# A hybrid image transformer: products in plain float32 in place of three products of split float32r parts

## Chip, cores, metric

The kernel runs on one core of a Trainium2 chip. The metric is the device time of one execution in microseconds, the median of three runs. Before the change it is 1892.42 us (1891.81 to 1893.7).

## What is computed

Two layers act on 512 image tokens ("l") and 256 context tokens ("c") of width 1024, all in float32. Cut to what matters:

```python
for l in range(2):
    need_ctx = l < 1                                  # layer 1 leaves the context as it is
    mod = silu(c) @ w_mod[l] + b_mod[l]               # shifts, scales, gates; the same for ctx
    h_l, h_c = modulate(rms_norm(x)), modulate(rms_norm(ctx))
    # token mixer: 2816 columns of w_in, split in eleven parts
    conv  = gated_short_conv(cb, cc, cx)              # 256 columns
    ret   = retention both ways, 4 heads of 64        # rq, rk, rv, two gates
    attn  = 8 heads of 64 on 2 key/value heads: keys in a window of 3 blocks of 128,
            plus 256 context tokens, plus a sink      # aq, ak, av
    x = x + g1 * (concat(conv, ret, attn) @ w_out[l])
    # 16 experts, each takes its 64 best tokens (32 of the context)
    a, u = xs @ w_gate[l, e], xs @ w_up[l, e]
    x = x + g2 * scatter((silu(a) * u) @ w_down[l, e] * gate)
    if need_ctx: ctx gets the same two updates
return rms_norm(x, final_g)
```

## The kernel before

Each layer has two stages. The **mixer stage** norms the tokens, turns them (features on partitions, `make_h`), multiplies by `w_in` in eleven projections of 256 columns (`proj`, in the order `ORDER`), runs attention (`attn_all`) and retention (`ret_gen`), and ends with the output projection (`out_proj`), the second norm, the router and the choice of tokens. In layer 0 the products with `w_mod` of both layers (`mod_gen`) lie in it too. The **expert stage** (`experts`) works through eight pairs of experts; the weights come through a ring of tiles of 2 MB (`Ring`), each pair needs 12 of them. `gate`, `up` and `down` multiply in column tiles of 32 columns (layer 0) or 64 columns (layer 1) of the array, so that two or four products stand in it at once (`lat_mm`, line 1133; `cx_mm`, line 1140). In layer 1 the tokens of a pair are gathered by a product with a one-hot matrix (`gather_pe`, line 1123) and a pair's result is added with another one-hot product (`add`, lines 1359 and 1360, and `last_pair`, lines 1165 and 1166); layer 0 scatters by DMA except for its last pair.

**Split products.** A product of the mixers is made of three. `split` (lines 275 and 276) rounds a float32 tile to float32r on ScalarE, H = round(src), and takes the rest L = src - H on VectorE or, every second time, on GpSimd. `mm3` (lines 354 to 356) adds H*H, L*H and H*L of the two operands into one PSUM tile. Weights are split two chunks at a time after their load (`split_w`, two buffers each for wH and wL); the tokens once per layer (`make_h`, lines 343 and 344); the mixers' results before the output projection (`split_m`, into mH and mL). Attention scores put H and L of a query on the two halves of the partitions and multiply by H of the keys (twice) and by L of the keys (lines 666, 667, 670, 671), the window's mask is added by a product of bfloat16 with the identity (lines 673, 675). The one-hot products take the result's two parts yH and yL.

The other products (retention, P times V at line 711, `w_mod` at line 201, experts, gather) are plain float32 already.

**Order.** Every engine runs its instructions in program order. In the mixer stage the program order comes from `weave`, which mixes the projections' steps with steps of attention, of retention and of `mod_gen` at fixed ratios; functions put in `later` (turning Q, K) run between a projection's chunks. Within the experts TensorE's order is written by hand. Loads are issued by SyncE in one queue; a load waits there until its tile is free. The `w_in`, `w_mod` and `w_out` loads share four tiles (`wraw`, `NW`). The ring has N0 + 4 + N2 = 1 + 4 + 3 tiles in layer 1 and 3 + N1 = 6 in layer 0; the first 3 or 4 of them open in the place of the mixers' tiles, in layer 0 before the second half of the output projection, when `split_m` is through (`ra_open`).

Of the kernel before, what the change touches and what calls it, by code (L numbers as in the profile page):

```python
# [23 lines left out]
F32R = mybir.dt.float32r  # L24
# [14 lines left out]
S2L = (11, 12)  # L39
# [5 lines left out]
NS = 2  # L45
# [5 lines left out]
SUB = 2  # L51
# [12 lines left out]
N0, N1, N2 = 1, 3, 3  # L64


def f32(ap):
    return ap.bitcast(F32)
# [21 lines left out]
def kernel(ctx_stack: ExitStack, tc: tile.TileContext, x, c, ctx, c_ctx, w_mod, b_mod, norm1_g,  # L90
# [23 lines left out]
    identb = cst.tile([128, 128], BF, name="identb")  # L114
    DVE.tensor_scalar(identb, jp, 0.0, None, op0=OP.is_equal)
    mprev = cst.tile([128, 128], BF, name="mprev")
    DVE.tensor_scalar(mprev, jp, 0.0, NEG, op0=OP.is_lt, op1=OP.mult)
    mnext = cst.tile([128, 128], BF, name="mnext")
# [67 lines left out]
    def mod_gen(l, wp, pp, groups):  # L186

        for b in groups:
# [4 lines left out]
            for k in range(KC):  # L193
                w = []
                for h in range(2):
                    w.append(wp.tile([128, 2, 512], F32, name="wm", tag="wraw", bufs=NW))
                    SP.dma_start(w[h], w_mod[l, 128 * k:128 * k + 128, 2048 * b + 1024 * h:2048 * b + 1024 * h + 1024]
                                 .rearrange("p (q n) -> p q n", q=2))
# [12 lines left out]
    def mod_half(wp, pp, hf):  # L211
# [5 lines left out]
        for k in range(0, KC, 2):  # L217
            ps = pp.tile([128, 512], F32, name="ps_mod", tag="t", bufs=4)
            for i in range(2):
                w = wp.tile([128, 2, 512], F32, name="wm", tag="wraw", bufs=NW)  # L220
# [45 lines left out]
    cnt = [0]  # L266
    later = []

    def sub_eng():
        cnt[0] += 1  # L270
        return POOL if cnt[0] % SUB == 0 else DVE

    def split(H, L, src):

        ACT.activation(H, src, AF.Copy)  # L275
        sub_eng().tensor_sub(L, src, f32(H))  # L276

    def x_tiles(st, load):

        xn = {}  # L280
        for s in "lc":
            for t, tag in enumerate(("rqTl", "rkTl", "gt1l", "cbl") if s == "l" else ("rkl", "rvl")):
# [29 lines left out]
    def x_ahead(p, pp, xn, hs):  # L312

        for j in range(KC):
            for s in "lc":
                n = 128 * NT[s]
                if s == "l" or j % 2 == 0:
                    hs[s, j] = p.tile([128, 512], F32, name="hsc", tag="s2", bufs=S2)
                    if s == "c":
                        hs[s, j + 1] = hs[s, j][:, n:]  # L320
                        hs[s, j] = hs[s, j][:, :n]
                ps = x_columns(pp, xn, s, j)
                if j % 2:
                    DVE.tensor_copy(hs[s, j], ps)
                else:
                    ACT.activation(hs[s, j], ps, AF.Copy)
            yield

    def make_h(l, p, pp, S, xn, hs, ss="lc"):

        for s in ss:
            S[s].hH = p.tile([128, KC, 128 * NT[s]], F32R, name="hH" + s)
            S[s].hL = p.tile([128, KC, 128 * NT[s]], F32R, name="hL" + s)
        for j in range(KC):
            for s in ss:
                A, B = A1[l][RI[s]], B1[l][RI[s]]
                if hs:
                    ps = h = hs[s, j]
                else:
                    ps = x_columns(pp, xn, s, j)  # L340
                    h = p.tile([128, 512], F32, name="hsc", tag="s2", bufs=S2)[:, :128 * NT[s]]
                DVE.tensor_scalar(h, ps, A[:, j:j + 1], B[:, j:j + 1], op0=OP.mult, op1=OP.add)
                ACT.activation(S[s].hH[:, j, :], h, AF.Copy)  # L343
                (DVE if s == "l" else POOL).tensor_sub(S[s].hL[:, j, :], h, f32(S[s].hH[:, j, :]))  # L344
            yield

    def split_w(w, src):
        wH = w.tile([128, 512], F32R, name="wH", tag="wH", bufs=NS)
        wL = w.tile([128, 512], F32R, name="wL", tag="wL", bufs=NS)
        split(wH, wL, src)  # L350
        return wH, wL

    def mm3(ps, aH, aL, bH, bL, start, stop):
        PE.matmul(ps, aH, bH, start=start, stop=False)  # L354
        PE.matmul(ps, aL, bH, start=False, stop=False)  # L355
        PE.matmul(ps, aH, bL, start=False, stop=stop)  # L356
# [6 lines left out]
    def proj(wq, pp, S, ss, l, c0, evac, transposed=False):  # L363

        acc = {}
        for kh in range(2):
# [139 lines left out]
    def alloc_streams(st, p, S, two):  # L506
        for s in "lc":
# [7 lines left out]
            X.akH = st.tile([128, 2, n], F32R, name="akH" + s)  # L515
            X.akL = st.tile([128, 2, n], F32R, name="akL" + s)
            for kv in range(2):
                POOL.memset(f32(X.akL[64 - 64 * kv:128 - 64 * kv, kv]), 0.0)
            X.av = st.tile([128, nt, 128], F32, name="av" + s)
        yield  # L520
        for s in "lc":
# [6 lines left out]
            if full:  # L528
                X.rqT = st.tile([128, 2, n], F32, name="rqT" + s, tag="rqT" + s)
                X.rkT = st.tile([128, 2, n], F32, name="rkT" + s, tag="rkT" + s)  # L530
                X.gt = [None, st.tile([128, nt, 256], F32, name="gt1" + s, tag="gt1" + s)]
                X.cb = st.tile([128, 2, n], F32, name="cb" + s, tag="cb" + s)

    def projections(l, w, wq, pp, S, st, need):
# [11 lines left out]
        def e_akav(s, i, ps):  # L546
            ACT.activation(S[s].av[:, 2 * i:2 * i + 2, :], ps[:, :, 128:256], AF.Copy)
            kt = evac_qk(w, ps[:, :, 0:128], i, 1.0, s == "l")
            kh = w.tile([128, 2, 2, 2, 64], F32R, name="kh", tag="s2", bufs=S2)
            kl = w.tile([128, 512], F32, name="kl", tag="s2", bufs=S2)[:, :256].rearrange("p (t n) -> p t n", t=2)  # L550
            for t in range(2):
                DVE.tensor_copy(kh[:, t], kt[:, t].rearrange("p (k d) -> p k d", k=2)[:, :, None, :]
                                .to_broadcast([128, 2, 2, 64]))
            for t in range(2):
                POOL.tensor_sub(kl[:, t].rearrange("p (k d) -> p k d", k=2),
                                kt[:, t].rearrange("p (k d) -> p k d", k=2), f32(kh[:, t, :, 0, :]))
            transposes(S[s].akH, i, lambda j, t: f32(kh[:, t, j]).rearrange("p a d -> p (a d)"))

            def f():
                tp = pp.tile([128, 2, 128], F32, name="ps_t", tag="t", bufs=4)  # L560
                for t in range(2):
                    PE.transpose(tp[:, t], kl[:, t], ident)
                for kv in range(2):
                    hs = slice(64 * kv, 64 * kv + 64)
                    DVE.tensor_copy(S[s].akL[hs, kv, 256 * i:256 * i + 256], tp[hs].rearrange("p t q -> p (t q)"))
            later.append(f)

        def queries(s, i, kv, g, q2):

            tp = pp.tile([128, 2, 2, 128], F32, name="ps_t", tag="t", bufs=4)  # L570
            for t in range(2):
                for j in range(2):
# [1333 lines left out]
```

## Time and profile before

| | |
|---|---|
| median of three runs | 1892.42 us (1891.81 to 1893.7) |
| the profiled execution | 1889.7 us, span 1887.9 us |
| TensorE busy | 1770.4 us, 94%, 12581 matmul instructions |
| VectorE / ScalarE / GpSimd busy | 655.8 / 479.8 / 329.9 us |
| granted TensorE clock, mean | 0.976 of 2.4 GHz |
| DMA | 528.42 MB, 280 GB/s over the span |

Busy time is the union of an engine's instructions. A matmul's duration runs from its start to its modelled end, through the array's depth, so that durations of neighbours overlap; how fast they follow each other is read from their starts. The type "f32" of a matmul's row stands for float32r too. "Idle before" is time in which the engine had no instruction running, with what ended it. A wait between engines is inferred from semaphores.

### The profile page before, as it was taken

Reading aid. Unit: us, or ns where it says so; the run is one execution under the profiler, and the core shown is the slowest. Engines: PE = TensorE matmul, PEld = TensorE weight load, DVE = VectorE, ACT = ScalarE, POOL = GpSimd, SP = SyncE. Lnnn points to the kernel's source line nnn. Section 1 sums busy time; section 2 is a strip of 40 time slices with the busy share of each in tenths; the row PEclk is TensorE's granted clock in tenths of the full one; section 3 lists DMA queues with packets and bytes.
Section 4 is the critical chain, followed back from the end, with each engine's and each line's share of the span. In section 5 each row is a group of like instructions: output and inputs, shape, how many; then the busy total and the mean of one; then the engine's idle time right before and its main releaser. Section 6 shows DMA issues by size and latency. Waiting matters only on the chain. (4 is left out here: it accounts for less than half of the span.)

```text
span 1887.9 us, 30047 instructions
## 1 busy us (share of the span) xinstructions
PE 1770.4 (94%) x12581; PEld 1018.5 (54%) x12581; DVE 655.8 (35%) x1671; ACT 479.8 (25%) x960; POOL 329.9 (17%) x341
## 2 busy tenths in 40 slices
PE   5899999999899999999999789899959999999995
PEld 2788877767533333333333688877745444534442
DVE  5645435673621001110001755446341122221224
ACT  3435434353411001010000446454331000000001
POOL 3323123333201011011001333322410000000001
PEclk9999999999899999999999899999979999999998
DMA  8454354257789999999998411111747999999995
GB/s 278 155 191 157 106 202 151 90 186 279 300 340 408 414 401 401 423 400 399 395 412 325 169 43 37 57 34 38 297 185 291 420 430 429 429 429 428 431 428 206
DMA packets 88919, 528.42 MB, mean 280 GB/s; under 512 B 9352, under 2 KB 31932, under 8 KB 64720
## 3 DMA queue, kind: packets, MB, share of 16 engines
q1 hardware_dynamic: 83040, 511.24, 68.0%
q0 software_dynamic: 5744, 15.26, 2.9%
q8 instruction: 99, 1.62, 0.3%
q14 instruction: 36, 0.29, 0.0%
HBM read 510.41 MB, written 16.06 MB: 279 GB/s over the span
## 5 line engine op out<-in xcount | busy, mean ns | idle before, releaser
L1133 PE MATMUL ps_g<-ring,xTl 128*32 128x512 f32 (+1 forms) x1472 | 238.0, 596 | 4.2 <-DMA ring<-in_w_gate_dram 3.0
L1133 PE MATMUL ps_u<-ring,xTl 128*32 128x512 f32 (+1 forms) x1536 | 233.1, 592 | 3.1 <-DMA ring<-in_w_up_dram 2.4
L1133 PE MATMUL ps_d<-ring,aT 128*32 128x512 f32 (+1 forms) x1536 | 234.6, 593 | 0.3 <-ACT sil L1241 0.3
L1270 ACT ACTIVATE aT<-ps_t 128x512 f32<-128x512 f32 x16 | 9.6, 598 | 619.0 <-PE ps_t L1266 578.1
L354 PE MATMUL acc<-wH,hHl 128*128 128x256 f32 x512 | 153.8, 301 | 2.7 <-ACT hHl L343 1.2
L1133 PEld LDWEIGHTS ps_g<-ring,xTl 128*32 128x32 f32 (+1 forms) x1472 | 72.7, 121 | 154.1 <-issue 137.5
L1133 PEld LDWEIGHTS ps_u<-ring,xTl 128*32 128x32 f32 (+1 forms) x1536 | 69.9, 119 | 153.1 <-issue 146.0
L355 PE MATMUL acc<-wH,hLl 128*128 128x256 f32 x512 | 147.0, 287 | 3.5 <-DVE hLl L344 3.4
L356 PE MATMUL acc<-wL,hHl 128*128 128x256 f32 x512 | 147.1, 287 | 1.1 <-DVE wL L276 1.1
L1133 PEld LDWEIGHTS ps_d<-ring,aT 128*32 128x32 f32 (+1 forms) x1536 | 70.4, 119 | 142.5 <-issue 136.7
L354 PEld LDWEIGHTS acc<-wH,hHl 128*128 128x128 f32 x512 | 99.7, 195 | 30.3 <-issue 23.7
L276 POOL TENSOR_TENSOR wL<-wraw,wH 128x512 fp32r<-128x512 f32 x44 | 57.5, 1308 | 275.0 <-ACT wH L275 263.8
L355 PEld LDWEIGHTS acc<-wH,hLl 128*128 128x128 f32 x512 | 99.8, 195 | 4.4 <-DVE hLl L344 4.4
L356 PEld LDWEIGHTS acc<-wL,hHl 128*128 128x128 f32 x512 | 99.8, 195 | 4.0 <-DVE wL L276 2.4
L1268 DVE COPY aT<-ps_t 128x512 f32<-128x512 f32 x16 | 11.1, 692 | 253.2 <-PE ps_t L1266 253.2
L1249 DVE TENSOR_TENSOR sil<-ps_u,sil 128x512 f32<-128x512 f32 x32 | 22.1, 692 | 220.8 <-PE ps_u L1133 220.8
L1185 POOL TENSOR_TENSOR x<-z,xTl 128x512 f32<-128x512 f32 x3 | 5.1, 1717 | 493.4 <-DVE x L1187 493.4
L678 DVE TENSOR_REDUCE mc<-ps_s 128x1 f32<-128x513 f32 (+2 forms) x80 | 55.2, 690 | 83.3 <-PE ps_s L675 52.1
L275 ACT ACTIVATE wH<-wraw 128x512 fp32r<-128x512 f32 x88 | 55.1, 629 | 95.6 <-PE acc L355 44.9
L680 ACT ACTIVATE P<-ps_s,mc 128x513 f32<-128x513 f32 (+2 forms) x80 | 55.1, 689 | 94.5 <-DVE mc L678 94.5
L1123 PE MATMUL ps_x<-OT,xn 128*128 128x128 f32 x512 | 67.0, 297 | 8.1 <-DVE OT L1115 8.1
L1123 PEld LDWEIGHTS ps_x<-OT,xn 128*128 128x128 f32 x512 | 65.3, 210 | 10.0 <-DVE OT L1115 8.5
(491 smaller groups left out, 3172.0 us busy)
## 6 DMA issues: line engine op xcount, KB each, us to landing
ring<-in_w_up_dram SPq DMA_DIRECT2D x62, 2048.0 KB, 16.6
ring<-in_w_gate_dram SPq DMA_DIRECT2D x61, 2048.0 KB, 13.3
ring<-in_w_down_dram SPq DMA_DIRECT2D x61, 2048.0 KB, 17.0
wm<-in_w_mod_dram SPq DMA_DIRECT2D x96, 512.0 KB, 4.6
wraw<-in_w_in_dram SPq DMA_DIRECT2D x44, 512.0 KB, 3.9
wraw_o<-in_w_out_dram SPq DMA_DIRECT2D x24, 512.0 KB, 4.1
ring<-in_w_gate_dram SPq DMA_DIRECT2D x12, 512.0 KB, 4.8
ring<-in_w_down_dram SPq DMA_DIRECT2D x12, 512.0 KB, 15.6
```

The lines of the kernel that those rows point to most:

```text
L275: ACT.activation(H, src, AF.Copy)
L276: sub_eng().tensor_sub(L, src, f32(H))
L354: PE.matmul(ps, aH, bH, start=start, stop=False)
L355: PE.matmul(ps, aL, bH, start=False, stop=False)
L356: PE.matmul(ps, aH, bL, start=False, stop=stop)
L678: DVE.tensor_reduce(mc[:, 0:1], sc, AX.X, OP.max, negate=True)
L680: ACT.activation(P[:, :nk + 1], sc, AF.Exp, bias=mc[:, 0:1], accum_out=mc[:, 1:2])
L1123: PE.matmul(ps[:, j], R.xn[:, t, c0:c0 + 128], OT[:, t], start=(t == 0), stop=(t == 3))
L1133: PE.matmul(G[h][c:c + n], lhs[:, k, c:c + n], W[e][:, j, 512 * h:512 * h + 512], start=(k == 0), stop=(k == KC - 1), tile_position=(0, c))
L1249: DVE.tensor_mul(sil[p][:, hs], U[h], sil[p][:, hs])
L1268: DVE.tensor_copy(aT[p][:, 4 * h:4 * h + 4], ps)
L1270: ACT.activation(aT[p][:, 4 * h:4 * h + 4], ps, AF.Copy)
```

## The change

`split`, `split_w`, `mm3`, `split_m` and all H and L tiles go. Each product of three (or two) parts is one plain float32 product on the unsplit tiles. `make_h` leaves h in one tile per stream, scaled on VectorE and ScalarE by turns. A query is turned once for two heads; K is kept with zeros in the other half of the partitions, once for each half. The masks and the identity they multiply are float32. The mixers' results (`S.o`, `S.cb`, `S.rqT`) live in a pool of their own (`mo`) and the output projection reads them there. The added result y is one tile. `w_mod` loads have four tiles of their own (`wm`), scratch tiles go from 11 and 12 to 20 and 24 (`S2L`), and the ring's tiles in layer 1 from 4 + 3 to 5 + 2 (`NA`, `N2`); the pool `ra` opens ahead of the output projection in both layers.

```diff
@@ proj
-                if j % 2 == 0:
-                    w2 = split_w(wq, raw[:, j:j + 2].rearrange("p j n -> p (j n)"))
-                wH, wL = (x[:, 256 * (j % 2):256 * (j % 2) + 256] for x in w2)
...
+                    h = S[s].h[:, k]
                     if transposed:
                         for i in range(2):
-                            mm3(acc[s][:, n * i:n * i + n], wH[:, 128 * i:128 * i + 128], wL[:, 128 * i:128 * i + 128],
-                                S[s].hH[:, k, :], S[s].hL[:, k, :], k == 0 and (n == 512 or i == 0),
-                                k == KC - 1 and (n == 512 or i == 1))
+                            PE.matmul(acc[s][:, n * i:n * i + n], raw[:, j, 128 * i:128 * i + 128], h,
+                                      start=k == 0 and (n == 512 or i == 0), stop=k == KC - 1 and (n == 512 or i == 1))
                     else:
                         for t in range(NT[s]):
-                            sl = slice(128 * t, 128 * t + 128)
-                            mm3(acc[s][:, 256 * t:256 * t + 256], S[s].hH[:, k, sl], S[s].hL[:, k, sl], wH, wL,
-                                k == 0 and t % 2 == 0, k == KC - 1 and t % 2 == 1)
+                            PE.matmul(acc[s][:, 256 * t:256 * t + 256], h[:, 128 * t:128 * t + 128], raw[:, j],
+                                      start=k == 0 and t % 2 == 0, stop=k == KC - 1 and t % 2 == 1)
@@ head
-            PE.matmul(sc[:, 256:512], q, C.akH[:, kv, :], start=True, stop=False)
-            PE.matmul(sc[:, 256:512], q, C.akL[:, kv, :], start=False, stop=True)
+            PE.matmul(sc[:, 256:512], q, C.ak[:, kv, a, :], start=True, stop=True)
             if nw:
-                PE.matmul(sc[:, 512:512 + nw], q, X.akH[:, kv, ks], start=True, stop=False)
-                PE.matmul(sc[:, 512:512 + nw], q, X.akL[:, kv, ks], start=False, stop=False)
+                PE.matmul(sc[:, 512:512 + nw], q, X.ak[:, kv, a, 128 * k0:128 * k1], start=True, stop=False)
                 if b:
-                    PE.matmul(sc[:, 512:640], identb, mprev, start=False, stop=b + 1 == X.nt)
+                    PE.matmul(sc[:, 512:640], ident, mprev, start=False, stop=b + 1 == X.nt)
@@ out_proj
-                wH, wL = next(ws)
+                w = next(ws)
                 for t in range(NT[s]):
                     ts = slice(128 * t, 128 * t + 128)
-                    mm3(acc[t, h], S.mH[:, k, ts], S.mL[:, k, ts], wH, wL, i == 0, i == KC - 1)
+                    m = S.o[(k - 4) // 2, t][:, k % 2] if k >= 4 else (S.cb, S.rqT)[k // 2][:, k % 2, ts]
+                    PE.matmul(acc[t, h], m, w, start=i == 0, stop=i == KC - 1)
@@ down
-                DVE.scalar_tensor_tensor(Dn[h], Dn[h], R.slot_l[:, 1, p:p + 1], R.g2[:, hs], op0=OP.mult, op1=OP.mult)
-                ACT.activation(yH[:, hs], Dn[h], AF.Copy)
-                DVE.tensor_sub(yL[:, hs], Dn[h], f32(yH[:, hs]))
+                DVE.scalar_tensor_tensor(y[:, hs], Dn[h], R.slot_l[:, 1, p:p + 1], R.g2[:, hs], op0=OP.mult, op1=OP.mult)
@@ add, and the same in last_pair
-                    PE.matmul(ps, o_, yH[:, hs], start=True, stop=False)
-                    PE.matmul(ps, o_, yL[:, hs], start=False, stop=True)
+                    PE.matmul(ps, o_, y[:, hs], start=True, stop=True)
@@ the kernel's body
-            ml_s, po_s, pc_s = ExitStack(), ExitStack(), ExitStack()
+            st_s.close()
+            po_s, pc_s = ExitStack(), ExitStack()
+            ra = [r1_s.enter_context(tc.tile_pool(name=f"ra{l}", bufs=1, side="left"))]
+            ring.more(ra[0], NA[l])
```

## Rows read from the trace of the kernel before

**Rows 1.** Stages: length, busy us (instructions) by engine, clock, DMA share, GB/s.

```profile
0.00:508.00 508.00, 471.01 (x3332) 360.69 (x3332) 277.51 (x779) 215.47 (x447) 158.06 (x181) 0.99 0.55 188
1042.00:1405.00 363.00, 318.86 (x2197) 267.16 (x2195) 196.72 (x531) 172.31 (x328) 111.97 (x112) 0.94 0.29 105
1405.00:1888.00 483.00, 449.62 (x2268) 212.58 (x2268) 110.41 (x211) 45.34 (x90) 5.07 (x3) 0.97 0.92 388
```

**Rows 2.** Timeline of PE, layer 0 mixers: start, us, engine, line, operation.

```profile
128.09 0.28 PE L354 MATMUL acc<-wH,hHl 128*128 128x256 f32 x1
128.21 0.28 PE L355 MATMUL acc<-wH,hLl 128*128 128x256 f32 x1
...
297.08 0.40 PE L354 MATMUL acc<-hHl,wH 128*128 128x512 f32 x1
297.32 0.39 PE L355 MATMUL acc<-hHl,wL 128*128 128x512 f32 x1
```

**Rows 3.** Timeline of PE in the experts, four and two column tiles, full width.

```profile
1035.31 3.62 PE L1140 MATMUL ps_dc<-ring,aTc 128*32 128x512 f32 x32
...
1581.62 7.52 PE L1123 MATMUL ps_x<-OT,xn 128*128 128x128 f32 x64 [1.33 <-DVE OT L1115]
1589.07 13.95 PE L1133 MATMUL ps_d<-ring,aT 128*64 128x512 f32 x64
```

**Rows 4.** PE by line and form (xcount | busy us, mean ns); one source.

```profile
L354 PE MATMUL acc<-wH,hHl 128*128 128x256 f32 x512 | 153.8, 301 | 2.7 <-ACT hHl L343 1.2 <-ACT wH L275 1.2 <-ACT P L680 0.2
L354 PE MATMUL acc<-wH,hHc 128*128 128x256 f32 x176 | 50.2, 285 | 0.0
L354 PE MATMUL acc<-wH,mHl 128*128 128x512 f32 x128 | 50.3, 399 | 2.5 <-DVE cbl L631 1.5 <-ACT mHl L275 1.0
L354 PE MATMUL acc<-hHl,wH 128*128 128x512 f32 x96 | 41.8, 435 | 0.8 <-ACT gt1l L627 0.8
L666 PE MATMUL ps_s<-akHc,q 128*128 128x256 f32 x80 | 24.6, 308 | 2.6 <-DVE mc L683 2.4
L354 PE MATMUL acc<-hHc,wH 128*128 128x256 f32 x48 | 13.8, 288 | 0.0
L354 PE MATMUL acc<-wH,mHc 128*128 128x512 f32 x32 | 13.6, 425 | 0.0
...
L670 PE MATMUL ps_s<-akHl,q x64: 274/333/414, 144.2 to 1307.2; 128*128 128x256 f32 x32, 128*128 128x384 f32 x32
```

**Rows 5.** One line group of splitting; a DMA issue with us to landing.

```profile
L275 ACT ACTIVATE wH<-wraw 128x512 fp32r<-128x512 f32 x88 | 55.1, 629 | 95.6 <-PE acc L355 44.9 <-DMA wraw<-in_w_in_dram 41.4 <-PE acc L356 9.1
...
wraw<-in_w_in_dram SPq DMA_DIRECT2D x44, 512.0 KB, 3.9
```

**Rows 6.** PE's waits in the two mixers: us in total, times, longest.

```profile
PE ps_t L1552 <- DMA rows<-in_final_g_dram: 14.2, 1, 14.2
...
PE ps_r L1012 <- DVE val L996: 9.7, 1, 9.7
PE ps_t L309 <- ACT xt L301: 5.7, 1, 5.7
```

**Rows 7.** A pair of layer 1: PE timeline, stretch, additions, waits.

```profile
1575.55 0.48 PE L1359 MATMUL ps_s<-yH,OH 128*128 128x512 f32 x1
1579.63 0.65 PE L1111 MATMUL ps_t<-tok_l,ident 16*128 16x64 f32 x4
...
1635.94 0.65 PE L1111 MATMUL ps_t<-tok_l,ident 16*128 16x64 f32 x4
...
1580.00:1636.30 56.30, 54.97 (x286) 25.86 (x286) 12.71 (x25) 4.60 (x9) 0.00 (x0) 1.00 1.01 429
...
L1361 DVE TENSOR_TENSOR x<-x,ps_s 128x512 f32<-128x512 f32 x56 | 34.0, 680 | 8.3 <-PE ps_s L1360 8.3
...
PE ps_g L1133 <- DMA ring<-in_w_gate_dram: 3.0, 2, 1.6
PE ps_u L1133 <- DMA ring<-in_w_up_dram: 2.4, 1, 2.4
```

More of the change, by code (lines that the diff above doesn't have):

```diff
@@ L38 @@
 NEG = -1e30
-S2L = (11, 12)
+S2L = (20, 24)
 S1 = 5
@@ L325, in x_ahead, with make_h @@
                 else:
-                    ACT.activation(hs[s, j], ps, AF.Copy)
+                    ACT.activation(S[s].h[:, j], ps, AF.Copy)
             yield
[L329 to L333, printed above, removed]
+    def make_h(l, pp, S, xn, ss="lc"):
         for j in range(KC):
             for s in ss:
-                A, B = A1[l][RI[s]], B1[l][RI[s]]
-                if hs:
-                    ps = h = hs[s, j]
-                else:
[L340 to L344, printed above, removed]
-            yield
@@ L347, in split_w @@
[L347 to L356, printed above, removed]
+                A, B = A1[l][RI[s]][:, j:j + 1], B1[l][RI[s]][:, j:j + 1]
@@ L358, in raw_load @@
+                h = S[s].h[:, j]
+                src = x_columns(pp, xn, s, j) if l else h
+                if (j % 2 == 0) == (s == "l"):
+                    DVE.tensor_scalar(h, src, A, B, op0=OP.mult, op1=OP.add)
+                else:
+                    ACT.activation(h, src, AF.Identity, scale=A, bias=B)
+            yield
     def raw_load(raw, l, kh, c0):
@@ L514, in alloc_streams @@
             X.q, X.o = {}, {}
[L515 to L518, printed above, removed]
+            X.ak = st.tile([128, 2, 2, n], F32, name="ak" + s)
+            for a in range(2):
+                POOL.memset(X.ak[64 - 64 * a:128 - 64 * a, :, a], 0.0)
             X.av = st.tile([128, nt, 128], F32, name="av" + s)
@@ new lines, in f @@
+                for j in range(2):
+                    for t in range(2):
+                        PE.transpose(tp[:, j, t], kd[:, t, j].rearrange("p a d -> p (a d)"), ident)
+                for a in range(2):
+                    hs = slice(64 * a, 64 * a + 64)
+                    src = tp[hs].rearrange("p j t q -> p j (t q)")
+                    if a:
+                        DVE.tensor_copy(S[s].ak[hs, :, a, 256 * i:256 * i + 256], src)
+                    else:
+                        ACT.activation(S[s].ak[hs, :, a, 256 * i:256 * i + 256], src, AF.Copy)
@@ new lines, in e_akav, with e_aq, g @@
+            later.append(f)
+        def e_aq(kv):
+            def f(s, i, ps):
+                qt = evac_qk(w, ps, i, 0.125, s == "l")
+                def g():
+                    tp = pp.tile([128, 2, 2, 128], F32, name="ps_t", tag="t", bufs=4)
+                    for t in range(2):
+                        for j in range(2):
+                            PE.transpose(tp[:, t, j], qt[:, t, 128 * j:128 * j + 128], ident)
+                    for t in range(2):
+                        b = 2 * i + t
+                        q = S[s].q[kv, b] = mx.tile([128, 2, 128], F32, name="q", tag=f"q{kv}{s}{b}")
+                        if t:
+                            ACT.activation(q, tp[:, t], AF.Copy)
+                        else:
+                            DVE.tensor_copy(q, tp[:, t])
+                later.append(g)
@@ L1314, in scatter @@
             if p == NACC - 1:
-                y2 = ep.tile([128, 2, D], F32R, name="yHL", tag="o00", bufs=1)
-                last.extend(y2[:, i] for i in range(2))
+                last.append(ep.tile([128, 2, D], F32, name="y", tag="o00", bufs=1)[:, 0])
                 xr = [ep.tile([128, 2, D], F32, name="xe", tag=f"o{g}", bufs=1) for g in ("01", "10", "11")]
@@ L1534 @@
             wq_s, p_s = ExitStack(), ExitStack()
+            mx = mx_s.enter_context(tc.tile_pool(name=f"mo{l}", bufs=1, side="right"))
             wq = wq_s.enter_context(tc.tile_pool(name=f"wq{l}", bufs=1, side="right"))
             p = p_s.enter_context(tc.tile_pool(name=f"pj{l}", bufs=1, side="right"))
+            for s in "lc":
+                S[s].h = p.tile([128, KC, 128 * NT[s]], F32, name="h" + s)
             with ExitStack() as s2:
@@ L1688, in fill @@
                 def fill(n):
-                    while not ra:
-                        yield
                     for _ in range(n):
@@ L1727, in passes @@
                                           () if nh else (g1_load["l"], lambda: x_load(xl, "l"))):
-                            for m in sm:
-                                next(m, None)
                             for _ in range(2):
```

204 lines of the change are left out of this document (46 added, 158 removed).

## The prediction

> **What bounds the kernel now.** I read the stage table first [rows 1]: the span falls into a mixer stage of layer 0 (0 to 508 us), its experts (to 1042), a mixer stage of layer 1 (to 1405) and its experts; the change touches the first, the third and the fourth. In the mixers TensorE (PE) is busy 471.0 of 508 and 318.9 of 363 us, while VectorE (DVE), ScalarE (ACT) and GpSimd (POOL) have half of that or less and DMA a share of 0.55 and 0.29. In the last stage DMA is at 0.92 and PE is nearly full too. The granted clock is 0.99, 0.94 and 0.97 there, so PE mostly runs at its upper level of 2.4 GHz.
>
> A busy PE need not be a full PE, because a matmul's duration holds its pipeline's depth. So next I read starts in the timeline. The three float32r products of a split follow each other every 0.118 us at 256 columns and every 0.234 us at 512 [rows 2]: 2.4 GHz at a little over one cycle per column. Plain float32 shows differently [rows 3]. It needs two instructions per product: L1123 stands as x64 where its loops make 32 products, and L1133 as x64 for the 32 of a matrix. Two column tiles: the 64 instructions at 1589.07 take 13.95 us, 31 rounds of 0.431 and a last duration of 0.593. Four column tiles: 32 in 3.62 us are 7 rounds of 0.433 and a last duration of 0.592. Since a round of two and of four tiles takes the same 0.43 us, the tiles run side by side, and 0.43 is the pace of one instruction of 512 columns: two cycles per column, four per product. At the full width of 128 columns the trace has it only with 128 moving columns (L1123): 64 in 7.52 us, 63 steps of 0.115; I take 0.112, since some of those starts wait for a PSUM bank.
>
> So in the mixers, where PE sets the pace, three passes become four, and what the splitting cost lies mostly on engines that have room.
>
> **The change part by part.** Prices: a float32 product is 2 x 0.218 = 0.436 us at 256 columns (half of 0.433 and the fixed few ns of the 0.112), 2 x 0.433 = 0.866 at 512, 2 x 0.112 = 0.224 at 128.
>
> (1) Projections and output projection. L354 counts the products [rows 4]: 512 + 176 + 48 = 736 at 256 columns, 128 + 96 + 32 = 256 at 512. Three parts cost 0.354 and 0.702. The difference is 736 x 0.082 = 60 us and 256 x 0.164 = 42 us: +102 us, by the counts of 576 and 416 some 59 in layer 0 and 43 in layer 1. No row shows a full-width float32 product over 128 columns. From above, float32r itself runs 10% over its columns (0.118 for 0.107), float32 in the rows 1 to 5% (0.431 for 0.427, 0.112 for 0.107); with 10% the instructions would be 0.235 and 0.470, and (1) grows by 736 x 2 x 0.017 + 256 x 2 x 0.037 = 44 us. From below, if such an instruction took as little as a float32r one, (1) would be -147 us; that is the rival A below. I take the pace of the column tiles, the nearest rows.
>
> The Trainium skill ("FP8 and Floating Point Precision", TensorE Precision Notes) says that true FP32 takes 4 passes through the array. By it, an estimate, a product is 4 x 256 / 2.4 GHz = 0.427 us and 0.853 us, and (1) would be 736 x 0.073 + 256 x 0.151 = +92 us where the rows give +102.
>
> (2) Scores: two float32r products on K's parts become one float32 product. 80 on the context and 32 on the window have 256 columns, 32 more 384 [rows 4]: 112 x (0.436 - 0.236) = 22 us; the 32 at 384: 2 x 0.327 - 2 x 0.176 (between the prices at 256 and 512) = 0.302 each, 10 us. +32 us.
>
> (3) Masks: 96 bf16 products become float32. Three of the four blocks have a left and three a right mask, for 8 heads and 2 layers. I take 128 columns at 2.4 GHz with float32r's overhead, 0.059 us, so 96 x (0.224 - 0.059) = +16 us; from above 96 x 0.224 = 22, from below 0.
>
> (4) Transposes: Q is turned once, not in two copies, for five pairs of blocks and two projections 40 instead of 80; the K remainders' 12 go: 52 at 0.112 = -6 us.
>
> (5) Splitting goes. ACT loses 88 copies of w_in's halves at 0.629 us [rows 5] and 48 of w_out's, 86 us, DVE and POOL as many subtractions, and besides those on h, K, Q and the mixers' results. None of these engines bounds a stage, so what counts is PE's waits for them. Bound from below: 0. From above: PE is idle 37.0 us in the first mixer and 44.1 in the second; of these 14.2 (the first load), 9.7 and 5.7 (top-k, the change of layer) have nothing to do with splitting [rows 6], which leaves 51. Hidden under the pipeline's depth, a wait of up to 0.16 us (0.28 less 0.118 [rows 2]) isn't counted as idle; 136 pieces with two parts each make at most 272 x 0.16 = 44 us more. So 0 to 95; I take 45, near the middle: a part of the idle time is the chains of rope, softmax and norms, which stay, but PE's longer products give these more time too. The clock is part of this: a mean of 0.94 in 363 us is 44 us at 1.2 GHz (363 x 0.06 / 0.5), and the longest idle stretches, top-k and the change of layer, stay; so I count nothing back for it, at most half of it, 22 us.
>
> (6) The added wait: PE now waits for a weight's DMA itself, and behind that product in its queue stand the woven scores, transposes and w_mod products, for which ACT's and DVE's softmax waits. But the load landed 3.9 us after its issue [rows 5] and is issued four slots ahead, two projections of over 10 us each; its slot is freed after the products instead of after the splitting. w_mod has slots of its own, off those of w_in on SP's queue. If this cover were gone, 44 + 24 loads would each show up to 4 us; PE's long waits in the mixers [rows 6] name DMA for the first load alone.
>
> (7) Expert stage of layer 1. Adding a pair's result takes PE from 1575.55 to 1579.63, 4.08 us for 8 products of two [rows 7]; with 8 x 0.866 = 6.93 it is +2.9 for each of 7 pairs, +20 us. DVE's additions (0.680 us each, 5.4 for 8) trail PE now and fit beside it then. Is that hidden by DMA? The next pair's turn ends its addition at 1635.94, so a period is 56.3 us, in which PE waits for no DMA; DMA needs 12 loads of 2.1 MB at 429 GB/s, 58.7 us. With +2.9 PE needs 59.2, just over that. PE's DMA waits in this stage sum to 3.0 + 2.4 = 5.4, some 6 with what the depth hides. So +20 - 6 = +14; bounds 0 (DMA still sets it) and +20.
>
> (8) Ends. The last pairs of layer 0 and 1 add with 12 and 8 products in front of what follows. At 0.40 us more each they would cost 8 us; but so far DVE's additions of 0.680 us [rows 7] set the pace, by 0.866 PE does, so it is 20 x 0.19 = 4 us. The copy to yH and the rest yL, 0.63 and 0.7 us, go from the front of layer 1's: -1. Together +3, bounds 0 and +8.
>
> (9) Pools: ring slots in layer 1 are 1 + 5 + 2 = 8 as before 1 + 4 + 3, in layer 0 six both times, opened half a pass earlier. The ring's loads then stand among those of w_out in SP's queue, which have four slots of lead. One ring slot is 2.1 MB, 4.9 us of DMA; I take 0, bounds -5 and +5. More scratch tiles: 0, covered by (5).
>
> Sum: 102 + 32 + 16 - 6 - 45 + 14 + 3 = +116 us. The profiled execution took 1889.7 (span 1887.9 and 1.8 around it), 2.7 under the median of 1892.42: 2006 for it, **2008 us** as a median.
>
> **Rivals.**
>
> A, not slower: at full width a float32 instruction streams one column per cycle, and the 0.112 us of L1123 is the weight load that it waits for. For it: no row shows a full-width one of over 128 columns. Against it: the column tiles' 0.43 us at two and at four tiles. Then (1) is -147, (2) 0, (7) 0 and the others 16 - 6 - 45 + 3: 1892 - 179 = 1713; but then the products that hide the other engines' chains are a third shorter, so that part of the relief isn't had, and I say 1750. It decides from an instruction of 1.52 times the float32r one (0.179 us at 256 columns), where the sum is zero; the column tiles show 1.85.
> The Trainium skill ("TensorE: Matmul & The Clock Gate", LDWEIGHTS) gives a weight load as columns / 1.2 GHz, for 128 some 0.107 us by my estimate; that is close to the 0.112 and so leaves A open as far as L1123 goes.
>
> B, relief in full: all 95 us of (5), 2008 - 50 = 1958, 1944 with (7) hidden and less where the clock gives back.
>
> C, full-width instructions with 10% overhead and little relief: +44 for (1), +5 each for (2) and (7), and 30 of the relief lost: 2092.
>
> D, PE waits for the weights' loads (6): 68 x 2 us, 2144.
>
> **How the numbers follow.** Forecast, 1965 to 2060: 0.64. A: 0.07. B: 0.14. C: 0.12. D: 0.03. The range 1950 to 2070 takes the forecast, most of B and the start of C. A measurement of this kernel can tell 0.2% (3.8 us) from nothing. Faster is A alone, 0.07; within 0.2% only an instruction close to A's 1.52 would be, 0.01; slower 0.92.
>
> **What would show it.** After: L1133 and L1123 unchanged; the projections with 1472 instructions at starts 0.218 us apart and 512 at 0.433; PE's share in the mixers up and these stages some 60 and 40 us longer; ACT and DVE down by a third there; a pair of layer 1 at about 59 us with no DMA waits. Starts of 0.12 us at 256 columns would make the prediction wrong and A right.

## The result, and the profile after

The changed kernel takes 1988.43 us (median of 4 runs, 1986.62 to 1989.86) where the kernel before takes 1892.12 (4 runs, 1890.63 to 1893.7): a ratio of 1.0508, 95% interval 1.049 to 1.0527, so 96.3 us slower. The forecast was 2008, +116, in a range of 1950 to 2070. The profiled execution took 1987.19 us with a span of 1985.4, 97.5 more than the span before; the rest of this section divides these 97.5.

First the head of the page: span, busy time by engine, and the shares of the chain that ended last.

```profile
span 1985.4 us, 27346 instructions
...
PE 1907.4 (96%) x11633; PEld 1001.6 (50%) x11633; DVE 546.9 (28%) x1507; ACT 364.7 (18%) x729; POOL 199.4 (10%) x221
...
PE 92%; DVE 3%; issue 2%; ACT 1%; DMA 1%; POOL 0%; SPq 0%; DVEq 0%; ACTq 0%; POOLq 0%
```

Then the stages, in the columns of [rows 1]: both mixers, the last stage, and within it the stretch from layer 1's first one-hot product to its last down product, of after and then of before.

```profile
0.00:568.00 568.00, 544.16 (x2773) 353.68 (x2773) 220.79 (x696) 157.96 (x327) 86.26 (x115) 0.99 0.50 172
1098.00:1500.00 402.00, 372.72 (x1819) 263.62 (x1818) 153.03 (x471) 127.05 (x236) 55.09 (x61) 0.97 0.27 95
1500.00:1985.00 485.00, 463.98 (x2268) 209.21 (x2268) 105.78 (x195) 35.78 (x74) 5.01 (x3) 0.98 0.92 386
1499.90:1961.30 461.40, 456.88 (x2252) 206.32 (x2252) 90.34 (x165) 28.65 (x57) 0.00 (x0) 1.00 0.95 401
```
```profile
1405.00:1864.50 459.50, 445.23 (x2252) 209.81 (x2252) 94.31 (x179) 37.03 (x71) 0.00 (x0) 0.98 0.96 403
```

In the mixers DVE, ACT and POOL did a fifth to a half less work (277.5 to 220.8, 215.5 to 158.0 and 158.1 to 86.3 us in layer 0), and yet the stages are 60 and 36 us longer: in layer 0 PE was busy for 471 us and now is for 544. The last stretch grew by 1.9 us only, although PE's busy time in it grew by 11.7.

The stages again, cut where PE starts the same product in each kernel (the last cut is where the last down product ends), for these two and for the experiments below (us of the profiled execution; layer 0's last addition stands at the front of layer 1's mixers):

| | mixers 0 | experts 0 | mixers 1 | experts 1 | end |
|---|---|---|---|---|---|
| before | 508.8 | 530.1 | 366.1 | 459.5 | 23.4 |
| after | 568.7 | 529.0 | 402.2 | 461.4 | 24.1 |
| e0_after | 567.7 | 527.6 | 403.7 | 462.6 | 24.1 |
| e8_double_out | 644.3 | 527.5 | 455.9 | 463.3 | 24.1 |
| e4_bf16_mask | 562.8 | 528.7 | 394.7 | 462.2 | 24.1 |
| e6_old_slots | 574.7 | 530.0 | 403.8 | 463.3 | 24.1 |
| e5_split_add | 570.4 | 528.9 | 402.1 | 459.5 | 23.4 |
| e1_one_piece | 502.2 | 529.9 | 350.7 | 461.5 | 23.4 |
| e2_wL_last | 509.4 | 529.1 | 369.0 | 459.4 | 23.4 |
| e3_ns3 | 509.1 | 530.0 | 364.7 | 462.7 | 23.4 |
| e9_plain_scores | 535.4 | 528.7 | 373.2 | 462.3 | 23.4 |
| e10_wL_dve | 512.9 | 528.7 | 354.6 | 460.1 | 23.4 |

Now the price of a product. The timeline of PE's mixers (start, us, engine, line, operation) has stretches without a gap.

```profile
469.70 6.60 PE L814 MATMUL acc<-wraw_o,o 128*128 128x512 f32 x15
...
1117.01 5.42 PE L346 MATMUL acc<-wraw,hl 128*128 128x256 f32 x24
```

Fifteen instructions over 512 columns take 6.60 us, of which the last one lasts its mean of 0.61 (the groups below): 14 steps of 0.428. Twenty-four over 256 columns take 5.42 with a last one of 0.38: 23 steps of 0.219. With two instructions a product costs 0.44 and 0.857 us at the full width of 128 columns. Three float32r products took 0.354 and 0.702 [rows 2], so plain float32 costs 1.23 times as much, and rival A, 0.12 us per instruction at 256 columns, is out.

The groups of PE's instructions by line and form, columns as in [rows 4]:

```profile
L346 PE MATMUL acc<-wraw,hl 128*128 128x256 f32 x1024 | 245.8, 384 | 0.1
L346 PE MATMUL acc<-wraw,hc 128*128 128x256 f32 x352 | 91.0, 380 | 0.0
L342 PE MATMUL acc<-hl,wraw 128*128 128x512 f32 x192 | 93.3, 608 | 0.0
L342 PE MATMUL acc<-hc,wraw 128*128 128x256 f32 x96 | 24.2, 383 | 0.0
L814 PE MATMUL acc<-wraw_o,o 128*128 128x512 f32 x160 | 74.7, 610 | 2.3 <-DMA wraw_o<-in_w_out_dram 2.3
L605 PE MATMUL ps_s<-akc,q 128*128 128x256 f32 x160 | 48.6, 386 | 1.3 <-DVE mc L619 1.2
L609 PE MATMUL ps_s<-mprev,ident 128*128 128x128 f32 x96 | 18.4, 274 | 0.0
```

L346 and L342 have 1024 + 352 + 96 = 1472 instructions over 256 columns, twice 736, and every multiply of the mixers stands with twice its count: two instructions per product, as forecast. The last column is the idle time before a group. The first of the three products, in the projections and the output projection, used to wait 6.0 us for ACT and DVE [rows 4]. The projections now wait 0.1, and in the output projection a weight's DMA shows up once, with 2.3.

PE's time in the two mixers, from each instruction's start to the next one's, sorted by the PSUM tile that it writes, puts the difference in its places (worked out over all instructions of both traces):

| PE's time by tile, us | before | after | difference | forecast |
|---|---|---|---|---|
| acc: projections, output projection | 500.1 | 564.1 | +64.0 | 102 - 45 = +57 |
| ps_s: scores and masks | 62.0 | 107.7 | +45.7 | 32 + 16 = +48 |
| ps_s: layer 0's last addition | 6.5 | 10.6 | +4.1 | +3 with the end |
| PE idle behind it (change of layer) | 5.7 | 3.5 | -2.2 | 0 |
| ps_t: transposes | 98.4 | 85.6 | -12.8 | -6 |
| ps_o (P times V) | | | -2.8 | 0 |
| others | | | about 0 | 0 |
| experts 0, experts 1, end (stages) | 1013.0 | 1014.5 | -1.1 +1.9 +0.7 | +14 |

So the two mixers together came out within some 6 us of the forecast, and the one large miss is in layer 1's experts.

### The profile page after: what moved, and what is told of

Read it like the earlier page. It is cut to its first block, busy times and chain, and to the rows that moved or that the text cites. A ratio compares the mean times of both kernels' runs of the same rounds, so it can differ in the third digit from the quotient of the medians.

```text
span 1985.4 us, 27346 instructions
## 1 busy us (share of the span) xinstructions
PE 1907.4 (96%) x11633; PEld 1001.6 (50%) x11633; DVE 546.9 (28%) x1507; ACT 364.7 (18%) x729; POOL 199.4 (10%) x221
## 4 chain that ended last, share of the span: by engine, by line
PE 92%; DVE 3%; issue 2%; ACT 1%; DMA 1%; POOL 0%; SPq 0%; DVEq 0%; ACTq 0%; POOLq 0%
PE acc L346 15%; PE ps_g L1068 11%; PE ps_d L1068 11%; PE ps_u L1068 11%; PE acc L814 6%; PE acc L342 5%; PE ps_x L1058 3%; PE ps_s L1283 3%; PE ps_gc L1075 3%; PE ps_uc L1075 3%; PE ps_dc L1075 3%; PE ps_o L647 2%; PE ps_mod L193 2%; PE ps_t L634 2%; PE ps_s L605 2%
## 5 line engine op out<-in xcount | busy, mean ns | idle before, releaser
L346 PE MATMUL acc<-wraw,hl 128*128 128x256 f32 x1024 | 245.8, 384 | 0.1
L346 PEld LDWEIGHTS acc<-wraw,hl 128*128 128x128 f32 x1024 | 187.5, 190 | 51.3 <-issue 28.7
L342 PE MATMUL acc<-hl,wraw 128*128 128x512 f32 x192 | 93.3, 608 | 0.0
L346 PE MATMUL acc<-wraw,hc 128*128 128x256 f32 x352 | 91.0, 380 | 0.0
L814 PE MATMUL acc<-wraw_o,o 128*128 128x512 f32 x160 | 74.7, 610 | 2.3 <-DMA wraw_o<-in_w_out_dram 2.3
L346 PEld LDWEIGHTS acc<-wraw,hc 128*128 128x128 f32 x352 | 66.6, 190 | 9.4 <-issue 0.6
L1075 PE MATMUL ps_dc<-ring,aTc 128*32 128x512 f32 x512 | 66.1, 592 | 0.0
L1058 PE MATMUL ps_x<-OT,xn 128*128 128x128 f32 x512 | 62.3, 284 | 3.7 <-DVE OT L1050 3.7
L1075 PE MATMUL ps_gc<-ring,xTc 128*32 128x512 f32 x512 | 65.4, 592 | 0.1
L1075 PE MATMUL ps_uc<-ring,xTc 128*32 128x512 f32 x512 | 65.3, 592 | 0.0
## 6 DMA issues: line engine op xcount, KB each, us to landing
ring<-in_w_down_dram SPq DMA_DIRECT2D x12, 512.0 KB, 15.4
```

The lines of the kernel that those rows point to most:

```text
L342: PE.matmul(acc[s][:, n * i:n * i + n], raw[:, j, 128 * i:128 * i + 128], h, start=k == 0 and (n == 512 or i == 0), stop=k == KC - 1 and ( ...
L346: PE.matmul(acc[s][:, 256 * t:256 * t + 256], h[:, 128 * t:128 * t + 128], raw[:, j], start=k == 0 and t % 2 == 0, stop=k == KC - 1 and t ...
L814: PE.matmul(acc[t, h], m, w, start=i == 0, stop=i == KC - 1)
L1058: PE.matmul(ps[:, j], R.xn[:, t, c0:c0 + 128], OT[:, t], start=(t == 0), stop=(t == 3))
L1075: PE.matmul(gcx[32 * b:32 * b + 32], lhs_c(k, e), W[e][:, j, 512 * h:512 * h + 512], start=(k == 0), stop=(k == KC - 1), tile_position=(0, ...
```

## The experiments

**Is PE the bound after the change, at 0.86 us per product of 512 columns?** With the output projection's products doubled the run must grow by their price, or by less if PE waits for others.

```diff
@@ out_proj, from the kernel after
-                    PE.matmul(acc[t, h], m, w, start=i == 0, stop=i == KC - 1)
+                    PE.matmul(acc[t, h], m, w, start=i == 0, stop=False)
+                    PE.matmul(acc[t, h], m, w, start=False, stop=i == KC - 1)
```

> The changed kernel, with each of the 160 products of the output projection done twice into the same PSUM tile (the result of that projection is doubled). If PE is the bound there and a product of 512 columns costs 2 x 0.433 us (theory), it takes 160 x 0.866 = 139 us more than the changed kernel, about 2127. If transfers or the norms between the passes set that stage (rival), less than 100 us of it is seen.

Measured: 2118.19 us, 1.1198 [1.1168, 1.1229] of the kernel before; 129.9 more than the kernel after's 1988.29 (e0_after). The trace has the doubled line at the same price and with no idle time before it:

```profile
L815 PE MATMUL acc<-wraw_o,o 128*128 128x512 f32 x160 | 82.6, 598 | 0.0
...
L814 PE MATMUL acc<-wraw_o,o 128*128 128x512 f32 x160 | 81.8, 593 | 0.0
```

The mixers of layer 1 grew by 53.7 us for 64 products, 0.839 each; those of layer 0 by 75.6 for 96, where the price gives 82. PE's pace sets both stages. Of the 7 us missing in layer 0, 2.6 are missing in the products written to acc and 3.2 in those written to ps_r, with their waits. Longer products probably fill gaps there that other engines' chains had left, but ps_r's time also differs by 4 us between the variants of the kernel after (6.3 to 10.4 us), so this isn't shown.

**The change's other half: the parts of it undone, one at a time.** Four runs: the kernel after again, its masks in bf16, layer 1's addition split as before, and the old scratch and load slots.

> The changed kernel once more, beside the runs of this call: 1988 us.

Measured: 1988.29 us, 1.052 [1.0503, 1.0536]. The difference repeats.

```diff
@@ masks, from the kernel after
-    mprev = cst.tile([128, 128], F32, name="mprev")
+    mprev = cst.tile([128, 128], BF, name="mprev")
...
-                    PE.matmul(sc[:, 512:640], ident, mprev, start=False, stop=b + 1 == X.nt)
+                    PE.matmul(sc[:, 512:640], identb, mprev, start=False, stop=b + 1 == X.nt)
```

> The changed kernel with the window's masks and the identity they multiply in bfloat16 again, as in the kernel before. If a mask's product costs its pace on PE (theory: 96 x 0.165 us), it takes 16 us less than the changed kernel, about 1972. If masks lie in PE's waits for the softmax (rival), it stays within 4 us of 1988.

Measured: 1974.35 us, 1.0443 [1.0425, 1.046], 13.9 less than with float32 masks. Sorted by tile, scores and masks lose 15.9 us. The masks' +16 was right within 2 us, for a matrix of zeros and -1e30 and one of zeros and ones.

```diff
@@ down, add and last_pair, from the kernel after, layer 1 only
-            y = last[0] if two else E[0].tile([128, D], F32, name="y", bufs=1)
+                    ACT.activation(yH[:, hs], Dn[h], AF.Copy)
+                    DVE.tensor_sub(yL[:, hs], Dn[h], yH[:, hs].bitcast(F32))
...
-                    PE.matmul(ps, o_, y[:, hs], start=True, stop=True)
+                        PE.matmul(ps, o_, y[:, hs], start=True, stop=False)
+                        PE.matmul(ps, o_, Y[p][1][:, hs], start=False, stop=True)
```

> The changed kernel, with the added result of layer 1's pairs split in two float32r parts again, as before. Theory: the plain product's 2.9 us more in each pair are given back by shorter waits for the one-hot tile behind DVE's additions, by DMA waits that go and by a clock that doesn't fall, so undoing it brings nothing: within 5 us of 1988, with DMA waits and dips of the granted clock back in layer 1's pairs. Rival (the prediction's own sum): PE's 7 x 2.9 us less the DMA waits count, 14 us less, about 1974.

Measured: 1987.6 us, 1.0517 [1.0498, 1.0537]: no difference from the kernel after. This is the term that failed. A pair of layer 1 in the kernel after, PE's timeline from one addition to the next:

```profile
1671.08 7.03 PE L1283 MATMUL ps_s<-y,OH 128*128 128x512 f32 x16
1678.04 0.65 PE L1046 MATMUL ps_t<-tok_l,ident 16*128 16x64 f32 x4
1679.15 7.52 PE L1058 MATMUL ps_x<-OT,xn 128*128 128x128 f32 x64 [0.46 <-DVE OT L1050]
1686.60 13.95 PE L1068 MATMUL ps_d<-ring,aT 128*64 128x512 f32 x64
...
1735.98 0.65 PE L1046 MATMUL ps_t<-tok_l,ident 16*128 16x64 f32 x4
```

And with the addition split again (e5_split_add) the steps around one gather:

```profile
1675.99 0.65 PE L1048 MATMUL ps_t<-tok_l,ident 16*128 16x64 f32 x4
1677.98 9.15 PE L1060 MATMUL ps_x<-OT,xn 128*128 128x128 f32 x64 [1.34 <-DVE OT L1052]
```

The addition takes 6.96 us (1671.08 to 1678.04) instead of 4.08 [rows 7], +2.9 as forecast. Then it gives back. With the split addition DVE's additions of 0.68 us trail PE, and the gather's one-hot tile OT comes behind them: from the index product to the gather it is 1.99 us, in the kernel after 1.11. Behind the longer halt the granted clock falls in some of the pairs. Windows of a gather: before (an idle of 1.34 us ends at 1637.93), then e5_split_add (one of 1.33 at 1620.5), then after (one of 0.46 at 1737.09), columns as in [rows 1].

```profile
1636.30:1638.00 1.70, 0.36 (x4) 0.23 (x3) 1.70 (x5) 0.00 (x0) 0.00 (x0) 0.96 1.01 434
1638.00:1641.40 3.40, 3.40 (x17) 3.40 (x17) 1.04 (x4) 0.00 (x0) 0.00 (x0) 0.52 1.01 422
1641.40:1643.00 1.60, 1.60 (x17) 1.60 (x16) 0.00 (x0) 0.00 (x0) 0.00 (x0) 1.00 1.03 440
```
```profile
1621.60:1625.00 3.40, 3.40 (x18) 3.40 (x18) 0.02 (x1) 0.00 (x0) 0.00 (x0) 0.51 0.99 424
```
```profile
1738.00:1741.40 3.40, 3.40 (x32) 3.40 (x32) 0.20 (x1) 0.33 (x1) 0.00 (x0) 1.00 0.99 424
```

At 0.52, the lower level of 1.2 GHz, PE starts 17 instructions in 3.4 us, at 1.00 it starts 32: a loss of 1.6 us. Five gathers stand behind an addition and halt for 1.33 to 1.34 us in the kernel before. At three of them the clock falls (1525, 1638 and 1757 us), in e5_split_add at four, in the kernel after at none. PE's waits in the stage, in the columns of [rows 6], first before, then after, then e5_split_add:

```profile
PE ps_x L1123 <- DVE OT L1115: 8.1, 8, 1.3
```
```profile
PE ps_x L1058 <- DVE OT L1050: 3.7, 8, 0.5
PE ps_g L1068 <- ACT xTl L1024: 1.1, 2, 0.6
```
```profile
PE ps_x L1060 <- DVE OT L1052: 8.1, 8, 1.3
PE ps_u L1070 <- DMA ring<-in_w_up_dram: 2.4, 1, 2.4
PE ps_g L1070 <- DMA ring<-in_w_gate_dram: 2.0, 1, 2.0
```

Sorted by tile, from start to start, the stage's +1.8 us is made up of the additions, +20.4, the index products with the halt at OT, -3.9, the gathers with their three stretches at half clock, -4.7, and gate, up and down, -10.0. Of these 10.0, 5.4 are the DMA waits of [rows 7]; 2.9 more lie in four gate matrices that take 0.5 to 1.1 us longer in the kernel before with little or no idle time to show for it. In place of unequal periods of 55.0 to 59.8 us, with waits for weights in some, the kernel after has four of 57.94 and one of 58.15, in which PE is idle for no more than the 0.46 us.

That says where PE gave the time back, not why it could. The stage's transfers say that. Windows from the stage's first one-hot product to the landing of its last weight, and from there to the end of the last down product, before and then after:

```profile
1405.00:1860.80 455.80, 441.54 (x2238) 208.82 (x2240) 93.55 (x178) 37.03 (x71) 0.00 (x0) 0.98 0.97 406
1860.80:1864.50 3.70, 3.69 (x16) 0.99 (x12) 0.76 (x1) 0.00 (x0) 0.00 (x0) 1.00 0.00 0
```
```profile
1500.00:1955.30 455.30, 450.84 (x2226) 204.53 (x2228) 89.49 (x164) 28.65 (x57) 0.00 (x0) 1.00 0.97 407
1955.30:1961.30 6.00, 6.00 (x29) 1.72 (x24) 0.75 (x1) 0.00 (x0) 0.00 (x0) 1.00 0.00 0
```

The last weight lands 455.8 us into the stage before and 455.3 after, and PE ends 3.7 and 6.0 us behind it. In all twelve traces it lands between 455.3 and 458.4 us, whatever PE does meanwhile: e2_wL_last has four stretches at half clock and DMA waits of 4.2 us, e3_ns3 one stretch and 8.5 us, and their stages take 459.4 and 462.7. So the transfers pace the stage in both kernels: the DMA share of a pair is 1.01 before [rows 7] and after, at 429 and 430 GB/s. PE had more room under them than its DMA waits, because halts and half clock filled a part of it, and the plain addition fits into that room but for 2 us. e5_split_add brings halts, half clock and DMA waits back and ends at the same time. No run changes the transfers themselves, so this cause is read from the traces alone.

```diff
@@ constants and w_mod's loads, from the kernel after
-S2L = (20, 24)
+S2L = (11, 12)
...
-                    w.append(wp.tile([128, 2, 512], F32, name="wm", tag="wm", bufs=NW))
+                    w.append(wp.tile([128, 2, 512], F32, name="wm", tag="wraw", bufs=NW))
```

> The changed kernel with the kernel before's memory: w_mod and w_in share four tiles again, scratch is 11 and 12 tiles instead of 20 and 24. Theory: this memory is not what the relief of the mixers came from; within 4 us of 1988. Rival: the additional tiles gave a part of it, 10 to 30 us more, about 2010.

Measured: 1993.79 us, 1.0543 [1.0525, 1.0561], 5.5 more than the kernel after, most of it (7 us in the profiled execution) in layer 0's mixers. The added memory is worth about 5 us of the relief; the forecast had it at nothing of its own. Sorted by tile, PE's time on the products with w_mod (ps_mod) goes from 56.9 to 62.4 us, which points to the tiles of w_mod's loads; scratch was not undone apart from them.

**Where did the 45 us of relief lie?** In the kernel before, the first run splits the first piece of the weights of each pool and uses its two parts for all the others, so that PE never waits for a weight's load or its splitting.

```diff
@@ split_w, from the kernel before
+        if id(w) in one:
+            return one[id(w)]
-        wH = w.tile([128, 512], F32R, name="wH", tag="wH", bufs=NS)
+        wH = w.tile([128, 512], F32R, name="wH", tag="wH", bufs=1)
...
+        one[id(w)] = wH, wL
```

> The kernel before, but a layer's weights are split once: every product of the projections and of the output projection uses the first split piece (the weights are left out of the computation, and with them 134 of 136 splits and PE's wait for them; the number of products and their sizes stay). If PE's waits for the weights' splitting are what the change gave back (theory: gaps between the three products sum to some 39 us in the two mixers), it takes 30 to 40 us less than before, about 1855. If splitting stood beside PE's work for nothing (rival), it stays within 5 us of 1892.

Measured: 1869.04 us, 0.9873 [0.9846, 0.99], -22.9. The stages' share of it: 6.6 us in layer 0's mixers, 15.4 in layer 1's. Sorted by tile, the products (acc) gain 13.2 and 11.4, and products written to ps_r lose 5.3 in layer 0. PE's waits for the weights and their splitting were real, at a good half of what the theory put on them; it is the single largest piece of the relief that an experiment shows. The run also takes the work of 134 splits off ACT, DVE and POOL, so it does not part PE's wait for a weight from what these engines' freed time does for other chains.

Two runs then ask whether that wait is one for the part wL, which comes last: in the first the products with wL stand behind all those with wH of the same piece, in the second wH has a third slot besides (NS = 3, paid for with a scratch tile each).

```diff
@@ proj and out_proj, from the kernel before
-                        for i in range(2):
-                            mm3(acc[s][:, n * i:n * i + n], wH[:, 128 * i:128 * i + 128], wL[:, 128 * i:128 * i + 128],
+                        for last in range(2):
+                            for i in range(2):
+                                if last:
+                                    PE.matmul(o, wL[:, cs], hH, start=False, stop=k == KC - 1 and (n == 512 or i == 1))
+                                else:
+                                    PE.matmul(o, wH[:, cs], hH, start=k == 0 and (n == 512 or i == 0), stop=False)
+                                    PE.matmul(o, wH[:, cs], hL, start=False, stop=False)
```

> The kernel before with the same three float32r products in another order: first wH with both token parts for all tiles of a chunk, then wL for all of them, so that wL is needed 0.9 to 1.9 us later. If PE waits for wL because its subtraction comes just after wH (theory: gaps of some 0.1 us before the second product, 18 us in all), it takes 8 to 18 us less, about 1880. If those gaps are the price of switching the stationary tile after a wait of any kind (rival), the gaps move to another place and it stays within 3 us.

> As the run with wL last, with three tiles for wH instead of two, and scratch of 10, 11 and 3 tiles in place of 11, 12 and 4. Theory: the copy to wH waits for the products that release its tile, and a third tile gives it the lead of one more piece; 5 to 15 us less than with wL last alone, about 1870. Rival: wL still has two tiles and binds in its place, no gain beside the run with wL last; or the smaller scratch costs as much.

Measured: 1892.88 us, 1.0003 [0.9988, 1.0019], and 1891.11, 0.9994 [0.998, 1.0008]. Neither gains. The small gaps that I had put down to wL, some 0.1 us ahead of the second product behind a switch from other work, stand at the same place when that product no longer uses wL: in e2_wL_last the two products with wH that follow a stretch of ps_s start 0.22 us apart (298.23 and 298.45 us), where the pace is 0.118. The order isn't it.

```diff
@@ sub_eng, from the kernel before
-        return POOL if cnt[0] % SUB == 0 else DVE
+        return DVE
```

> The kernel before with every subtraction of the splitting on VectorE, none on GpSimd, where it takes 1.31 us in place of 0.71 us. Theory: with the shorter split PE's waits for weights shrink by a third, 5 to 8 us less, about 1885. Rival: the subtractions delay the softmax's own work on VectorE by as much, within 4 us of 1891 or slower.

Measured: 1883.36 us, 0.9956 [0.9943, 0.997], 8.6 us faster: the engine is it, in part. The run moves the subtractions on the mixers' results too. The sources of the weights' subtraction, min/median/max ns, in the kernel before and with all on DVE:

```profile
L276 POOL TENSOR_TENSOR wL<-wraw,wH x44: 1263/1291/1594, 34.5 to 1318.3; 128x512 fp32r<-128x512 f32 x44
L276 DVE TENSOR_TENSOR wL<-wraw,wH x44: 675/692/1608, 36.0 to 1313.3; 128x512 fp32r<-128x512 f32 x44
```
```profile
L276 DVE TENSOR_TENSOR wL<-wraw,wH x88: 660/692/1530, 36.0 to 1311.0; 128x512 fp32r<-128x512 f32 x88
```

On POOL a subtraction takes 1.29 us, on DVE 0.69. The gain lies in layer 1's mixers (-11.5 us); layer 0's lost 4, for a reason that I did not look into.

**Do the shorter chains of Q and K give anything back?** The kernel before, with K and Q and the scores as in the kernel after and all else split as it was.

```diff
@@ head, from the kernel before
-            PE.matmul(sc[:, 256:512], q, C.akH[:, kv, :], start=True, stop=False)
-            PE.matmul(sc[:, 256:512], q, C.akL[:, kv, :], start=False, stop=True)
+            PE.matmul(sc[:, 256:512], q, C.ak[:, kv, a, :], start=True, stop=True)
```

> The kernel before with the attention scores alone in plain float32: Q turned once and K not split, as in the changed kernel, the masks still bfloat16 and all other products still three. By the sum's terms +32 us for the scores and -6 us for the transposes. Theory: the chains that end in split Q and K (copy, subtraction, two turns) hold PE up in layer 1 and give 8 to 12 us back, so +14 to +18, about 1907. Rival: nothing is given back here, +26, about 1917.

Measured: 1924.45 us, 1.0166 [1.0152, 1.018], +32.5; my theory's figure was too low, and so was the rival's. By tile the scores cost +31.9 (+17.1 and +14.8), the +32 of the forecast; the transposes gave 8.9, and the other lines took about as much (acc +3.7, ps_mod +2.1, ps_o +3.7). The edit also drops the hold by which the second Q projection waited until the first four heads' attention was issued (`need("at0")`), as the kernel after does. The shorter chains relieve nothing on net as long as the weights are split.

## Why the prediction was right, step by step

(1) Priced as measured: at 0.438 and 0.857 us, 736 and 256 products are 542 us against 440 by [rows 2, 4], +102. The choice of the column tiles' pace [rows 3] for a full width that no row showed was the decision of the case, and it held; the bounds either side of it, A and C, did not. Rule and row agree here: the 4 passes of the Trainium skill ("FP8 and Floating Point Precision", TensorE Precision Notes) give an estimate of 0.427 and 0.853, 2.5% and 0.5% under the trace.

(2), (3) and (8) were +48 and +3 and came to +45.7 and +4.8 in the tables; e9_plain_scores (+31.9) and e4_bf16_mask (13.9) show the first two one by one.

(4) was -6, 52 turns at 0.112 us. e9_plain_scores shows -8.9 for the same edit: from start to start, the kernel before takes 18.2 us for the 116 turns of Q and K, 0.157 each with their waits, and e9_plain_scores 9.7 for 64. The kernel after takes 7.4 for them, and -12.8 over all transposes.

(5) was -45 between 0 and 95. The products' time without any stall leaves 500.1 - 440 = 60 us lost before and 564.1 - 542 = 22 after: 38 of relief there. With the -2.8 of P times V, the -2.2 at the change of layer and the transposes' 4 to 7 beyond their price it is 47 to 50. Taking the middle was a choice and not a derivation, and that it came so close is luck in part. The place was right: PE was idle for 37.0 and 44.1 us in the two mixers and is for 24.1 and 29.3. Half of what stays, 26.7 us, is what the forecast named, the first load, top-k and the change of layer. PE's longest waits in the mixers after:

```profile
PE ps_t L1477 <- DMA rows<-in_final_g_dram: 13.5, 1, 13.5
...
PE ps_r L947 <- DVE val L931: 9.7, 1, 9.7
PE ps_t L291 <- ACT xt L283: 3.5, 1, 3.5
```

About 23 us of it are traced to the weights (e1_one_piece) and about 5 to memory (e6_old_slots). These are single edits on two kernels, and need not add. The remaining 19 to 22 are open: splitting of h and of the mixers' results, and longer products that cover other chains (at most 7 us of such cover in e8_double_out), were not tried apart.

(6) was 0: the DMA of a mixer's weight shows up once, with 2.3 us, where rival D wanted 68 times 2.

(7) is the step that failed: +14 forecast, +1.9 measured, 12 of the 19 us by which the sum was too high (scores, masks, transposes, P times V and the change of layer came out 14 lower, the products 7 higher). Its price of 2.9 us a pair was right. I had taken PE's DMA waits of 5.4 us as all the room that PE had under the transfers, and so had PE set the pace. The last weight's landing, 455.8 us into the stage before and 455.3 after, shows that the transfers set it in both kernels: the term's own lower bound, 0 because DMA still sets it, is nearly what came. The room that I missed was in the halts and the half clock. Yet [rows 7] showed DVE's additions of 0.680 trailing, the very thing that makes OT late, and [rows 3] showed the gather with 1.33 us of idle time before it; I named the first and didn't follow it to the next pair, and counted no clock for the second.

(9) as forecast for the ring: layer 1's DMA waits went and, but for one of 0.3 to 0.9 us in e0_after and three of its variants, no others came.

So the answer to the rivals: A and C by the price of a product, D by the waits; B (1958, or 1944 with (7) hidden) shared its mechanism with the forecast; half of the bound of 95 was had, and (7) was hidden nearly in full.

## What to carry to other kernels

Count a plain float32 product as two instructions of two cycles per column at 2.4 GHz, as it comes out at 128, 256 and 512 columns here (0.112, 0.219 and 0.428 us), and three float32r passes at one cycle per column and their measured 10% overhead (0.118 us at 256 columns): that is a factor of 1.23. An engine that is already full pays all of it, while the work taken from the others returns only what the full engine had waited for them. Before crediting that relief, take the suspected wait away by itself; e1_one_piece came nearest to that. A cheap move of the same work to a faster engine (e10_wL_dve, 1883.36 us) was the only version here that computes everything and beat both kernels. And where an engine gets more work in a stage that is also full of transfers, look first at when the last transfer lands: the longer products of layer 1's experts cost 2 of their 20 us, because the transfers gave the pace and PE's halts had hidden how much room it had under them.

## What the runs showed of the hardware

- With four column tiles, two, or none, a float32 instruction over 512 columns starts every 0.43 us (side by side in the tiles); over 256 columns at full width every 0.219.
- A halt of 1.33 to 1.35 us of PE before a gather was followed by some 3.5 us at a granted clock of about 0.5 in three of five pairs of the kernel before, and in 18 of the 35 such halts of the seven traces with split additions. None followed the 49 halts of 0.44 to 0.46 us in the twelve traces. In layer 1's experts a busier PE ran at a mean of 1.00 instead of 0.98.
- The expert stage of layer 1 reads its last weight 455.3 to 458.4 us after its start in all twelve traces, with one to four such stretches at half clock or none: what PE lost to the clock there, the stage did not pay.
- The same subtraction, 128x512 from float32 to float32r, takes 1.29 us on POOL and 0.69 on DVE, and its place there cost 8.6 us of the whole run.
